# Three edits to a one-layer decoder step: late squares of the second norm, two squares of the first norm summed by TensorE, two projection outputs side by side

## The chip, the cores and the metric

The kernel runs on one core of a Trainium2 chip. The engines are TensorE (PE in the profile; PEld is its weight load), VectorE (DVE), ScalarE (ACT), GpSimd (POOL) and SyncE (SP), which issues most of the loads. Each engine works through its own list of instructions in order and waits for others by semaphores. The metric is the device time of one execution in microseconds, the median of several runs. What a core's memory for matmul results holds is called PSUM; it has eight banks, and a tile of the kernel takes one or two of them.

## The reference, cut to what matters

One layer of a decoder step on 576 tokens (512 of a new sequence, 64 of eight running ones), 1024 channels, all in float32:

```
xn = rms_norm(h, g_mix);  z = xn @ w_in                      # 6 x 1024 columns
h  = h + (gate_a * (conv(...) @ w_out_conv) + gate_b * pool(...)) @ w_o
hn = rms_norm(h, g_mlp)
h  = h + square(relu(hn @ w_up)) @ w_down                    # 4096 wide
h  = h + sigmoid(rms_norm(h, g_ple) @ w_ple_gate) * (p @ w_ple_proj)
return rms_norm(h, g_final), ...                             # and the new states
```

`rms_norm(x, g)` is `x * rsqrt(mean(x * x) + 1e-6) * g`. There are four of these norms. The first and the second are the ones that the change touches.

## The kernel before, in words

Activations lie with the channels on the partitions: eight chunks `xs[j]` of 128 channels by 576 tokens, the tokens in two halves of 288. For accuracy each float32 operand is split into a high and a low part (`split`, lines 88 and 89: ScalarE casts the high part, VectorE subtracts it), and each product takes three matmuls (high x high, high x low, low x high). A weight half, 128 x 512, is loaded by SP into `wraw` (eight buffers), split into `wsp` (NF = 7 slots), and used. `stream.take(n)` hands out the next n halves and sees to it that the splits run up to seven halves and the loads six further ahead; with `live`, it counts halves handed out earlier that are still in use. The halves of `w_up` are partly sums of two loads, the second of them issued from GpSimd's queue (line 149).

A norm is spread over the work around it. The gain g is folded into the operands, and the factor 1/rms per token is applied to the products or to the outputs later. `Rms.add` squares a chunk on ScalarE (line 307) and adds it on GpSimd to the first square (line 311), so that one sum tile remains in `parts`. `Rms.tokens` sums that tile over the partitions with matmuls against a column of ones, one for each of six groups of 96 tokens (line 320, twelve TensorE instructions), takes the root on ScalarE (line 324) and refines its reciprocal on VectorE (lines 325 to 329). `Rms.spread` brings the result back to all partitions with six small matmuls (line 336), and `copies` puts it into SBUF.

First norm (lines 351 to 361): the eight chunks are squared as they arrive, TensorE works through chunk k of the first three products (`psf`), and after k = 5 come the sums, after k = 6 the spreading.

Projection with `w_o` (lines 591 to 602): the operands `merged` are eight split chunks; the last two come out of the pooling gates just before. For each of eight outputs x TensorE runs 48 matmuls (8 chunks x 3 x 2 halves) into two banks. VectorE adds the result to `xs[j]` (line 596), ScalarE applies the gain (`gx`, line 599), and after each second output `hg.add` makes the seven operands of the next stage from the pair (lines 514 to 525, tiles `gx` and `gt`). Then the chunk is squared for the second norm.

MLP (lines 608 to 657): four blocks b of 1024 columns. The product with `w_up` is done with seven quarter products in place of eight (`pairs_of`); one pair is seven quarters of twelve matmuls. In the first block, pair 0 is written in a late order: three of the four chunks are used first, and what needs the last operands (`rest`) comes behind. `finish` applies the squared ReLU and splits the result; `between(q)` runs after pair q and holds, in block 0, the second norm's sums (q = 0) and its spreading (q = 1). Its result `r2s` is used only in the last block (line 654). There are six banks in this stage.

A planner orders each engine's list before the run by costs and the availability of buffers, with program order as its priority. An instruction can so be moved ahead of its place in the text. From the projection on, every matmul issued through the helper `matmul` is kept behind the TensorE instruction that was written before it; the norm's own matmuls are not kept so, but the matmul written next is kept behind them.

Of the kernel before, what the change touches and what calls it, by code (L numbers as in the profile page):

```python
# [9 lines left out]
AF = mybir.ActivationFunctionType  # L10
# [3 lines left out]
D = 1024  # L14
NJ = D // P
# [3 lines left out]
NH = 2  # L19
# [23 lines left out]
def tile_hybrid_step(ctx: ExitStack, tc: tile.TileContext, x, pt, vecs, rc, ident, sconv, spool, w_first, w_in,  # L43
                     w_pool, w_oc, w_o, w_up, w_down, w_pg, w_pp,
                     y_out, ncp, npp, ncs, nps):
    nc = tc.nc
# [19 lines left out]
    def bank():  # L66
        return banks.tile([P, 512], F32, tag="b", name="b")[:, :HT]
# [28 lines left out]
    def split_act(src, scale=None):  # L96
        return split(src, [P, NH, HT], acts, "act", scale)

    def mm(outs, w, c, m, act, start, stop):

        wh, wl = (t[:, c % KH:c % KH + m] for t in w[c // KH])
        for i, (wt, at) in enumerate(((wh, act[0]), (wh, act[1]), (wl, act[0]))):
            for o, cols in outs:
                matmul(o, wt, cols(at), start=start and i == 0, stop=stop and i == 2)

    def both(ps):
        return [(ps[h] if isinstance(ps, list) else ps[:, h, :HT], lambda t, h=h: t[:, h, :]) for h in range(NH)]

    def steps(ps, unit, operands, ks, base=0, m=P, step=P, first=None, last=None):
        for k in ks:  # L110
            mm(both(ps), unit, base + k * step, m, operands[k], k == first, k == last)

    def product(unit, operands, base=0, m=P, step=P):

        ps = psum.tile([P, NH, 512], F32, tag="ps", name="ps") if banks is None else [bank() for _ in range(NH)]
        n = len(operands)
        steps(ps, unit, operands, range(n), base, m, step, 0, n - 1)
        return ps
# [101 lines left out]
    halved = [i + h * NQ for i in range(NQ) for h in range(2)]  # L220
# [16 lines left out]
    stream = Stream(order)  # L237
# [5 lines left out]
    def v(i, j):  # L243
        return vec[:, i, j:j + 1]

    xall = const.tile([P, NJ, NH, HT], F32, tag="xall", name="xall")
    xs = [xall[:, j] for j in range(NJ)]
# [12 lines left out]
    epst = const.tile([P, 1], F32, tag="epst", name="epst")  # L260
# [10 lines left out]
    xg, first = [], []  # L271
# [24 lines left out]
    class Rms:  # L296
# [2 lines left out]
            self.shape = [P, n, width]  # L299
            self.at = [(h, c) for h in range(n) for c in range(0, width, chunk)]  # L300

        def add(self, t, last=False):
            sq = tmp.tile(self.shape, F32, tag="t", name="sq")
            if last:
                nc.vector.tensor_tensor(out=sq, in0=t, in1=t, op=ALU.mult)
            else:
                nc.scalar.activation(sq, t, AF.Square)  # L307
            if last or not self.parts:
                self.parts.append(sq)
            else:  # L310
                nc.gpsimd.tensor_tensor(out=self.parts[0], in0=self.parts[0], in1=sq, op=ALU.add)  # L311

        def tokens(self):

            n, m = len(self.at), self.chunk
            self.ps = ps = psum.tile([P, NH, 512], F32, tag="ps", name="psn")
            sums = ps[:m, 0, self.width:self.width + n]
            for i, (h, c) in enumerate(self.at):
                for k, a in enumerate(self.parts):
                    nc.tensor.matmul(  # L320
                        sums[:, i:i + 1], a[:, h, c:c + m], ones32[:, 0:1],
                        start=k == 0, stop=k == len(self.parts) - 1)
            rt, ms, y, t = (tmp.tile([m, n], F32, tag=g, name=g, bufs=2) for g in ("rt", "ms", "ry", "rz"))
            nc.scalar.activation(rt, sums, AF.Sqrt, bias=epst[:m], scale=1.0 / D)
            nc.vector.tensor_scalar(out=ms, in0=sums, scalar1=1.0 / D, scalar2=EPS, op0=ALU.mult, op1=ALU.add)
            nc.vector.reciprocal(y, rt)
            nc.vector.tensor_tensor(out=t, in0=y, in1=y, op=ALU.mult)
            nc.vector.scalar_tensor_tensor(out=t, in0=t, scalar=-0.5, in1=ms, op0=ALU.mult, op1=ALU.mult)
            nc.vector.scalar_tensor_tensor(out=y, in0=t, scalar=1.5, in1=y, op0=ALU.add, op1=ALU.mult)
            self.y = y  # L330
# [19 lines left out]

    stat = Rms()
    for j in range(NJ):
        stat.add(xs[j])
    ps0 = [psum.tile([P, NH, 512], F32, tag="ps", name="psf") for _ in range(3)]
    for k in range(NJ):
        for u in range(3):
# [51 lines left out]
    for j in range(NJ):  # L408
        ps = product(stream.take(2), xg)
# [5 lines left out]
    for j in range(NJ):  # L415
        ps = product(stream.take(2), ya_in)
# [3 lines left out]
    merged = []  # L420
    for g, w in enumerate(WINDOWS):
        pooled = []
        for i in range(2):
            j = 2 * g + i
            ps = product(stream.take(2), xg)
# [13 lines left out]
            while d < w:  # L439
                q = tmp.tile([P, PEXT], F32, tag="ext", bufs=4, name="q")  # L440
# [23 lines left out]
        for i in range(2):  # L464
            ps = product(stream.take(2), xg)
# [6 lines left out]
        for i in range(2):  # L472
            j = 2 * g + i
            ps = product(wp, pooled, base=i * P, step=2 * P)
            t = tmp.tile([P, NH, HT], F32, tag="t", name="t")
# [15 lines left out]
    def quarter(o, w, bs, ks, start, stop):  # L491
        for k in ks:
            wh, wl = (t[:, k * P:(k + 1) * P] for t in w)
            hi, lo = bs[k]
            for i, (wt, at) in enumerate(((wh, hi), (wh, lo), (wl, hi))):
                matmul(o, wt, at, start=start and k == 0 and i == 0,
                       stop=stop and k == NQ - 1 and i == 2, skip_group_check=True)

    class Operand:

        def __init__(self):
# [25 lines left out]
    def pairs_of(n, op, corner, finish, late=False, between=None):  # L527
# [17 lines left out]
        for i in range(n):  # L545
# [41 lines left out]
            if between:  # L587
                between(i)


    stat = Rms()
    hg = Operand()
    for x, j in enumerate(halved):
        ps = product(stream.take(2), merged)
        for h in range(NH):
            nc.vector.tensor_tensor(out=xs[j][:, h], in0=ps[h], in1=xs[j][:, h], op=ALU.add)
        if x % 2 == 0:
            g = tmp.tile([P, 4, HT], F32, tag="g", name="gx", bufs=2)
        nc.scalar.mul(g[:, 2 * (x % 2):2 * (x % 2) + 2], xs[j], v(G_MLP, j))
        if x % 2:  # L600
            hg.add(x // 2, g)
        stat.add(xs[j])


    accs = [None] * NJ
# [2 lines left out]
    for b in range(NFB):  # L608
        sq = [None] * NJ

        def corner(q, g, c11):
            nc.scalar.activation(g[:, 1], c11, AF.Relu)

        def finish(q, g):
            nc.scalar.activation(g[:, 0], g[:, 0], AF.Relu, scale=-1.0)
            nc.scalar.activation(g[:, 2:4], g[:, 2:4], AF.Relu)
            nc.scalar.activation(g, g, AF.Square)
            sq[q] = split_act(g[:, 0:2])
            sq[q + NQ] = split_act(g[:, 2:4])

        def between(q):
            if b == 0 and q == 0:
                stat.tokens()
            if b == 0 and q == 1:
                stat.r2s = stat.copies(stat.spread(), "r", "rs")[1]

        pairs_of(NQ, hg, corner, finish, b == 0, between)
        r2s = stat.r2s
        if b == NFB - 1:
            pp = []  # L630
            for k in range(2):
                t = tmp.tile([P, NH, HT], F32, tag="t", name="pin")
                nc.sync.dma_start(t, pt[:, k])
                pp.append(split_act(t))
        for j in range(NJ):
            if j == 0:
                two = [stream.take(2), stream.take(2, live=2)]
                two = [(w, [bank() for _ in range(NH)]) for w in two]
                for ks in (halved[:-2], halved[-2:]):
                    for w, ps in two:  # L640
                        steps(ps, w, sq, ks, first=halved[0], last=halved[-1])
            if j < 2:
                ps = two[j][1]
            else:
                ps = product(stream.take(2), sq)
            if b == 0:
                accs[j] = keep.tile([P, NH, HT], F32, tag="keep", name="acc")
                for h in range(NH):
                    nc.scalar.copy(accs[j][:, h], ps[h])
                continue  # L650
            for h in range(NH):
                nc.vector.tensor_tensor(out=accs[j][:, h], in0=ps[h], in1=accs[j][:, h], op=ALU.add)
            if b == NFB - 1:
                nc.vector.tensor_tensor(out=accs[j], in0=accs[j], in1=r2s, op=ALU.mult)
                nc.vector.tensor_tensor(out=xs[j], in0=accs[j], in1=xs[j], op=ALU.add)
                hg2.append(split_act(xs[j], v(G_PLE, j)))
                stat3.add(xs[j])
# [3 lines left out]
    for i in range(2):  # L661
        w = stream.take(2)
        for m in range(NJ // 2):
            ps = product(w, pp, base=2 * m * P)
            t = keep.tile([P, NH, HT], F32, tag="keep", name="proj")
# [25 lines left out]
    for h, (a, b) in enumerate(((0, cut), (cut, NT))):  # L691
        for j in range(NJ):
            if h == 0:
                gate_w.append(stream.take(2))
            ps = psum.tile([P, NH, 512], F32, tag="ps", name="psg")
# [106 lines left out]
```

## Time and profile before

| | |
|---|---|
| median of the runs | 912.74 us (three runs, 911.63 to 913.75) |
| the profiled execution's own time | 914.41 us |
| span of its instructions | 912.6 us |
| TensorE busy | 892.8 us (98%) |
| VectorE, ScalarE, GpSimd busy | 524.6, 375.2, 114.3 us |
| mean granted TensorE clock | 0.987 of full speed |

In the lines of a timeline the columns are start in us, duration in us, engine, source line, operation, written tile and what it reads, shapes, and how many instructions were merged; in brackets stand the idle time of the engine before it and what ended it. A matmul's duration overlaps with the next one's: what it costs is the distance between two starts. In the view by windows the columns are the stretch in us, its length, the busy time and number of instructions of PE, PEld, DVE, ACT and POOL, the granted clock of TensorE, the share of the DMA engines and GB/s.

### The profile page before, as it was taken

Reading aid. Unit: us, or ns where it says so; the run is one execution under the profiler, and the core shown is the slowest. Engines: PE = TensorE matmul, PEld = TensorE weight load, DVE = VectorE, ACT = ScalarE, POOL = GpSimd, SP = SyncE. Lnnn points to the kernel's source line nnn. Section 1 sums busy time; section 2 is a strip of 40 time slices with the busy share of each in tenths; the row PEclk is TensorE's granted clock in tenths of the full one; section 3 lists DMA queues with packets and bytes.
Section 4 is the critical chain, followed back from the end, with each engine's and each line's share of the span. In section 5 each row is a group of like instructions: output and inputs, shape, how many; then the busy total and the mean of one; then the engine's idle time right before and its main releaser. Section 6 shows DMA issues by size and latency. Waiting matters only on the chain.

```text
span 912.6 us, 16574 instructions
## 1 busy us (share of the span) xinstructions
PE 892.8 (98%) x6650; PEld 890.1 (98%) x6650; DVE 524.6 (57%) x880; ACT 375.2 (41%) x642; POOL 114.3 (13%) x150
## 2 busy tenths in 40 slices
PE   8999999999999999999899999999999999999995
PEld 8999999999999999999799999999999999999995
DVE  7654544423335767857785327733773467687555
ACT  8232222322212323344575336721573157546432
POOL 5000000000002211012200110001100110021353
PEclk9999999999999999999799999999999999999997
DMA  8422222222222222333443535444544454333002
GB/s 271 138 83 82 81 82 82 86 89 83 83 82 82 81 82 83 107 96 87 110 127 126 136 96 148 129 104 106 139 137 107 110 123 135 96 98 94 18 23 83
DMA packets 52653, 93.66 MB, mean 103 GB/s; under 512 B 6240, under 2 KB 9952, under 8 KB 52576
## 3 DMA queue, kind: packets, MB, share of 16 engines
q1 hardware_dynamic: 47824, 84.18, 29.3%
q0 software_dynamic: 4608, 8.39, 5.9%
q8 instruction: 52, 0.85, 0.4%
q14 instruction: 25, 0.20, 0.1%
q10 hardware_dynamic: 144, 0.03, 0.0%
HBM read 89.60 MB, written 2.99 MB: 101 GB/s over the span
## 4 chain that ended last, share of the span: by engine, by line
PE 93%; DVE 2%; ACT 2%; DMA 1%; issue 1%; POOL 1%; SPq 0%; DVEq 0%; ACTq 0%; POOLq 0%
PE b L62 47%; PE ps L62 38%; PE psg L62 6%; PE psf L62 1%; DMA xall<-x 1%; ACT hi L88 1%; PE psn L320 1%; PE psn L336 1%; POOL sq L311 0%; ACT hi L91 0%; DMA raw<-w_pg 0%; DVE lo L89 0%; ACT sq L307 0%; DVE gt L523 0%; DVE xall L684 0%
## 5 line engine op out<-in xcount | busy, mean ns | idle before, releaser
L88 ACT CAST hi<-raw 128x512 fp32r<-128x512 f32 x290 | 178.9, 620 | 389.1 <-PE ps L62 206.0
L89 DVE TENSOR_TENSOR lo<-raw,hi 128x512 fp32r<-128x512 f32 x290 | 205.0, 711 | 144.0 <-ACT hi L88 140.4
L62 PE MATMUL b<-lo,hi 128*128 128x288 f32 x1120 | 277.4, 297 | 2.9 <-DVE lo L89 2.9
L62 PE MATMUL b<-hi 128*128 128x288 f32 x1120 | 277.3, 297 | 2.6 <-ACT hi L88 1.6
L62 PE MATMUL b<-hi,lo 128*128 128x288 f32 x1120 | 277.0, 296 | 0.0
L62 PEld LDWEIGHTS b<-lo,hi 128*128 128x128 f32 x1120 | 193.4, 189 | 3.4 <-DVE lo L89 3.4
L62 PEld LDWEIGHTS b<-hi 128*128 128x128 f32 x1120 | 193.4, 189 | 3.1 <-ACT hi L88 1.8
L62 PEld LDWEIGHTS b<-hi,lo 128*128 128x128 f32 x1120 | 193.5, 189 | 0.0
L62 PE MATMUL ps<-hi 128*128 128x288 f32 x880 | 188.5, 296 | 0.0
L62 PE MATMUL ps<-lo,hi 128*128 128x288 f32 x880 | 188.4, 296 | 0.0
L62 PE MATMUL ps<-hi,lo 128*128 128x288 f32 x880 | 188.4, 296 | 0.0
L62 PEld LDWEIGHTS ps<-hi 128*128 128x128 f32 x880 | 141.8, 189 | 0.0
L62 PEld LDWEIGHTS ps<-lo,hi 128*128 128x128 f32 x880 | 141.8, 189 | 0.0
L62 PEld LDWEIGHTS ps<-hi,lo 128*128 128x128 f32 x880 | 141.8, 189 | 0.0
L149 POOL DMA_DIRECT2D raw<-w_up x32 | 27.9, 871 | 326.7 <-DMA raw<-w_up 194.8
L311 POOL TENSOR_TENSOR sq<-sq 128x576 f32<-128x576 f32 (+2 forms) x34 | 44.3, 1303 | 119.6 <-ACT sq L307 70.5
L62 PE MATMUL psg<-hi 128*128 128x320 f32 (+1 forms) x128 | 38.1, 298 | 0.7 <-ACT r L343 0.7
L62 PE MATMUL psg<-lo,hi 128*128 128x320 f32 (+1 forms) x128 | 37.9, 296 | 0.0
L62 PE MATMUL psg<-hi,lo 128*128 128x320 f32 (+1 forms) x128 | 37.9, 296 | 0.0
L89 DVE TENSOR_TENSOR lo<-s,hi 128x512 fp32r<-128x512 f32 x32 | 24.1, 752 | 12.4 <-ACT hi L88 11.6
L169 DVE TENSOR_TENSOR s<-raw 128x512 f32<-128x512 f32 x16 | 12.0, 748 | 32.5 <-DMA raw<-w_up 32.4
L307 ACT ACTIVATE sq<-xall 128x576 f32<-128x576 f32 (+2 forms) x39 | 22.6, 585 | 18.1 <-DVE xall L713 18.1
(124 smaller groups left out, 719.3 us busy)
## 6 DMA issues: line engine op xcount, KB each, us to landing
raw<-w_in SPq DMA_DIRECT2D x90, 256.0 KB, 2.7
raw<-w_up SPq DMA_DIRECT2D x80, 256.0 KB, 2.9
raw<-w_down SPq DMA_DIRECT2D x64, 256.0 KB, 2.9
raw<-w_up POOLq DMA_DIRECT2D x32, 256.0 KB, 4.5
raw<-w_oc SPq DMA_DIRECT2D x16, 256.0 KB, 2.7
raw<-w_o SPq DMA_DIRECT2D x16, 256.0 KB, 2.7
raw<-w_pg SPq DMA_DIRECT2D x16, 256.0 KB, 3.1
xall<-x SPq DMA_DIRECT2D x7, 288.0 KB, 6.1
```

The lines of the kernel that those rows point to most:

```text
L62: i = nc.tensor.matmul(*args, **kw)
L88: nc.scalar.copy(hi, src)
L89: nc.vector.tensor_tensor(out=lo, in0=src, in1=as32(hi), op=ALU.subtract)
L149: nc.gpsimd.dma_start(raw, y, accum_op=ALU.add)
L169: nc.vector.tensor_tensor(out=p.rs2, in0=p.rs1, in1=p.ra, op=ALU.add)
L307: nc.scalar.activation(sq, t, AF.Square)
L311: nc.gpsimd.tensor_tensor(out=self.parts[0], in0=self.parts[0], in1=sq, op=ALU.add)
L320: nc.tensor.matmul(sums[:, i:i + 1], a[:, h, c:c + m], ones32[:, 0:1], start=k == 0, stop=k == len(self.parts) - 1)
L336: nc.tensor.matmul(self.ps[:, h, c:c + m], self.y[:, i:i + 1].broadcast_to([m, P]), idt[:m, :m], start=True, stop=True)
```

## The change: what it does

- First norm: the last two of the eight squares are no longer added by GpSimd. They stay as parts of their own, and `tokens` sums three tiles with TensorE where it summed one.
- Projection: a helper `two_products` makes two products side by side, over all chunks but the last two for both, and then over the last two. The same order stood in the `w_down` loop before and is now a function; it is used also for the first two outputs with `w_o`.
- Second norm: the last two squares are taken out of the projection loop and put behind pair 0 of the first block, `tokens` is put behind pair 1 and the spreading behind pair 2. The two squares and the root are kept behind the ScalarE instruction written before them (`pin`).

```diff
-        def add(self, t, last=False):
+        def add(self, t, last=False, part=False, pin=False):
...
-                nc.scalar.activation(sq, t, AF.Square)
-            if last or not self.parts:
+                i = nc.scalar.activation(sq, t, AF.Square)
+                if pin:
+                    tc.keep_in_program_order(i)
+            if last or part or not self.parts:
                 self.parts.append(sq)
...
-            nc.scalar.activation(rt, sums, AF.Sqrt, bias=epst[:m], scale=1.0 / D)
+            i = nc.scalar.activation(rt, sums, AF.Sqrt, bias=epst[:m], scale=1.0 / D)
+            if pin:
+                tc.keep_in_program_order(i)
...
     for j in range(NJ):
-        stat.add(xs[j])
+        stat.add(xs[j], part=j >= NJ - 2)
...
+    def two_products(operands, ks):
+
+        two = [(w, [bank() for _ in range(NH)]) for w in (stream.take(2), stream.take(2, live=2))]
+        for part in (ks[:-2], ks[-2:]):
+            for w, ps in two:
+                steps(ps, w, operands, part, first=ks[0], last=ks[-1])
+        return [ps for _, ps in two]
...
+    opened = two_products(merged, range(NJ))
     for x, j in enumerate(halved):
-        ps = product(stream.take(2), merged)
+        ps = opened[x] if x < 2 else product(stream.take(2), merged)
...
-        stat.add(xs[j])
+        if x < NJ - 2:
+            stat.add(xs[j])
...
             if b == 0 and q == 0:
-                stat.tokens()
+                for j in halved[-2:]:
+                    stat.add(xs[j], pin=True)
             if b == 0 and q == 1:
+                stat.tokens(pin=True)
+            if b == 0 and q == 2:
                 stat.r2s = stat.copies(stat.spread(), "r", "rs")[1]
...
-                two = [stream.take(2), stream.take(2, live=2)]
-                two = [(w, [bank() for _ in range(NH)]) for w in two]
-                for ks in (halved[:-2], halved[-2:]):
-                    for w, ps in two:
-                        steps(ps, w, sq, ks, first=halved[0], last=halved[-1])
+                two = two_products(sq, halved)
```

More of the change, by code (lines that the diff above doesn't have):

```diff
@@ L311, in add, with tokens @@
                 nc.gpsimd.tensor_tensor(out=self.parts[0], in0=self.parts[0], in1=sq, op=ALU.add)
-        def tokens(self):
+        def tokens(self, pin=False):
             n, m = len(self.at), self.chunk
@@ L636, in tile_hybrid_step @@
             if j == 0:
-                two = [stream.take(2), stream.take(2, live=2)]
-                two = [(w, [bank() for _ in range(NH)]) for w in two]
-                for ks in (halved[:-2], halved[-2:]):
-                    for w, ps in two:
-                        steps(ps, w, sq, ks, first=halved[0], last=halved[-1])
+                two = two_products(sq, halved)
             if j < 2:
-                ps = two[j][1]
+                ps = two[j]
             else:
```

## The prediction

> **What bounds the kernel now.** I read the page's first part, then the clock in windows, then the timelines around the gaps. From the page:
>
> ```profile
> PE 892.8 (98%) x6650; PEld 890.1 (98%) x6650; DVE 524.6 (57%) x880; ACT 375.2 (41%) x642; POOL 114.3 (13%) x150
> ```
>
> TensorE is busy 98% of the span, so only two things can be won: its idle time, 912.6 - 892.8 = 19.8 us in all, and time in which its clock is low. The view by windows (length, busy time and instructions of PE, PEld, DVE, ACT, POOL, then the granted clock) shows where the clock is low:
>
> ```profile
> 22.00:25.40 3.40, 1.52 (x15) 1.52 (x16) 3.40 (x5) 1.55 (x2) 1.83 (x1) 0.96 0.37 122
> 25.40:28.80 3.40, 3.40 (x17) 3.40 (x17) 2.51 (x9) 0.00 (x0) 0.00 (x0) 0.54 0.89 288
> ...
> 441.60:445.00 3.40, 1.38 (x8) 0.79 (x6) 3.12 (x7) 2.82 (x5) 0.78 (x2) 1.00 0.60 198
> 445.00:448.40 3.40, 0.92 (x4) 0.82 (x4) 3.33 (x4) 1.51 (x4) 1.53 (x2) 0.50 0.78 155
> 448.40:451.80 3.40, 3.40 (x20) 3.40 (x19) 2.44 (x4) 2.66 (x4) 0.00 (x0) 0.50 0.15 57
> 451.80:455.20 3.40, 3.40 (x16) 3.40 (x15) 0.44 (x2) 0.62 (x1) 0.88 (x1) 0.50 0.24 77
> ...
> 465.00:470.00 5.00, 5.00 (x40) 5.00 (x39) 4.36 (x9) 2.71 (x7) 0.00 (x0) 1.00 0.72 177
> ```
>
> After 3.4 us with only 1.52 or 1.38 us of PE work, the clock is at half for one stretch at the first norm and for three at the second. The two places in PE's timeline, second norm first:
>
> ```profile
> 441.72 0.29 PE L62 MATMUL b<-hi,lo 128*128 128x288 f32 x1
> 443.62 0.40 PE L62 MATMUL b<-hi 128*128 128x288 f32 x1 [1.60 <-ACT hi L88]
> 444.43 0.40 PE L62 MATMUL b<-lo,hi 128*128 128x288 f32 x1 [0.42 <-DVE lo L89]
> ...
> 447.58 0.61 PE L62 MATMUL b<-lo,hi 128*128 128x288 f32 x1 [2.48 <-DVE lo L89]
> ...
> 448.71 0.44 PE L62 MATMUL b<-hi,lo 128*128 128x288 f32 x1
> 448.95 1.97 PE L320 MATMUL psn<-ones,sq 128*96 128x1 f32 x12
> 450.77 0.59 PE L62 MATMUL b<-hi 128*128 128x288 f32 x1
> ...
> 455.23 0.29 PE L62 MATMUL b<-hi 128*128 128x288 f32 x1
> 455.36 0.29 PE L62 MATMUL b<-lo,hi 128*128 128x288 f32 x1
> ```
>
> Three waits, 4.5 us together, for splits of the last operands of the first pair; then 23 matmuls (counted in the timeline) and the norm's sums run from 447.58 to 455.23 at half clock (0.24 us from start to start, as 448.71 to 448.95; 0.13 at full clock, as 455.23 to 455.36; over longer stretches 0.1325). What makes the operands late:
>
> ```profile
> 434.19 0.45 DVE L523 TENSOR_TENSOR gt<-gx,gt 128x288 f32<-128x288 f32 x1
> ...
> 437.23 0.68 DVE L89 TENSOR_TENSOR lo<-raw,hi 128x512 fp32r<-128x512 f32 x1
> ...
> 438.09 0.67 ACT L307 ACTIVATE sq<-xall 128x576 f32<-128x576 f32 x1
> ...
> 438.66 1.12 ACT L88 CAST hi<-raw 128x512 fp32r<-128x512 f32 x2
> ...
> 438.91 1.42 POOL L311 TENSOR_TENSOR sq<-sq 128x576 f32<-128x576 f32 x1 [4.15 <-ACT sq L307]
> ...
> 439.30 1.59 DVE L89 TENSOR_TENSOR lo<-raw,hi 128x512 fp32r<-128x512 f32 x1 [1.39 <-ACT hi L88]
> ...
> 440.81 0.81 DVE L596 TENSOR_TENSOR xall<-b,xall 128x288 f32<-128x288 f32 x2
> ...
> 442.33 0.67 ACT L307 ACTIVATE sq<-xall 128x576 f32<-128x576 f32 x1
> ...
> 442.91 0.66 ACT L88 CAST hi<-gx 128x576 fp32r<-128x576 f32 x1
> ...
> 444.67 2.19 DVE L523 TENSOR_TENSOR gt<-gx,gt 128x288 f32<-128x288 f32 x1
> ...
> 444.83 1.70 POOL L311 TENSOR_TENSOR sq<-sq 128x576 f32<-128x576 f32 x1
> ```
>
> The squares of the last two chunks stand in ScalarE's queue ahead of the casts TensorE waits for, and each GpSimd addition stretches a VectorE instruction beside it: 0.68 becomes 1.59, and 0.45 becomes 2.19.
>
> **The change part by part.** (1) Late squares. Without the square at 438.09 the weight casts behind it start 438.66 - 438.09 = 0.57 earlier; without the addition at 438.91 the VectorE split takes 0.68 in place of 1.59, 0.91 less. So the last chunk's sum (440.81) and all behind it come 1.48 earlier. The cast at 442.91 also loses the square ahead of it (442.91 - 442.33 = 0.58), ends near 441.4, and TensorE, free at 441.85, no longer has the first wait (1.60). Next is the low part of the same operand: VectorE works without a gap there, so 444.43 only becomes 442.95; a wait of about 1.0 remains. Then the 2.19 becomes 0.45, 1.74 less, and the last resumption, 447.58, becomes 447.58 - 1.48 - 1.74 = 444.36, behind a wait of about 0.9.
>
> The norm's sums leave this place. They come back behind the second pair at full clock, where the first norm's 12 instructions took 24.92 - 23.88 = 1.04 (rows below). What is left here are the 23 matmuls. In 441.6 to 445.0 TensorE now stands 1.9 of 3.4 us, so is busy about 1.5: nearest to 1.38 and 1.52, after which the clock fell. I take one stretch at half clock: 4.8 matmuls until 445.0, 14.2 in the 3.4 us at 0.24, the last 4 in 0.53, end 448.9 instead of 455.23: 6.3 won, less 1.04, **5.3 us**. Bounds: without a fall, 444.36 + 23 x 0.1325 = 447.4, 7.8 less 1.04, 6.8; with a second stretch another 3.4 x (1 - 0.1325/0.24) = 1.5 less, 3.8; and nothing, if other work fills the place (rivals).
>
> The Trainium skill ("TensorE: Matmul & The Clock Gate", Part 1) says that the clock halves after an idle window of about 3.4 us and returns after a busy one. The stretches above agree in length, but the two windows before the falls were not idle, so the rule as it stands is too mild; by it the 6.8 would hold.
>
> (2) What is moved and must be hidden. Two squares (0.67 each), two additions (1.42 and 1.70), the table load and the root go behind the first and second pair; the spreading of the result a pair later, same work. The casts which the squares are pinned behind, and where TensorE needs the sums:
>
> ```profile
> 463.85 0.67 ACT L88 CAST hi<-g 128x576 fp32r<-128x576 f32 x1
> ...
> 470.74 1.47 PE L336 MATMUL psn<-idt,ry 96*128 96x96 f32 x12
> ...
> 474.62 0.67 ACT L88 CAST hi<-g 128x576 fp32r<-128x576 f32 x1
> ```
>
> Squares from 464.5, additions done near 468: 2.7 before TensorE ends the second pair (470.74). The root waits for sums already there; behind it ScalarE's casts stand up to the load's 1.3 longer, covered by weights split ahead. The additions again stretch VectorE, by up to 2 x 1.74 = 3.5 us, in a stretch where it is busy 4.36 of 5; no matmul waits for VectorE there, so I cost it at 0, and at 3.5 if that cover were gone. The Trainium skill ("SBUF — State Buffer", section on the two separate sides) has VectorE and GpSimd share one port pair under an exclusive lock when a VectorE operation has two SBUF inputs; the 2.19 agrees, and by it the price moves with the additions and doesn't vanish. The two loads of the per-layer inputs on SP take the squares' buffers and so shift with them; weight loads behind them run six ahead: 0.
>
> (3) Two squares of the first norm by TensorE.
>
> ```profile
> 17.66 3.77 POOL L311 TENSOR_TENSOR sq<-sq 128x576 f32<-128x576 f32 x2 [1.05 <-ACT sq L307]
> ...
> 21.17 0.43 PE L62 MATMUL psf<-hi,lo 128*128 128x288 f32 x2
> ...
> 21.87 1.96 POOL L311 TENSOR_TENSOR sq<-sq 128x576 f32<-128x576 f32 x1
> ...
> 23.88 1.18 PE L320 MATMUL psn<-ones,sq 128*96 128x1 f32 x12 [2.29 <-POOL sq L311]
> ...
> 24.92 0.65 PE L62 MATMUL psf<-hi 128*128 128x288 f32 x2
> ...
> 28.92 1.48 PE L336 MATMUL psn<-idt,ry 96*128 96x96 f32 x12
> ```
>
> The last two of seven additions go (half the 3.77, and 1.96); the fifth ends near 19.6, before TensorE is free, so the wait of 2.29 goes. But three parts make 36 instructions of 12: 36 x 1.04/12 = 3.12. Start 23.88 - 2.29 = 21.59, end 24.71 against 24.92: **0.2 us**. Whether the clock then falls as before is open: a stretch with twelve such sums and eight matmuls (448.40) did not raise it, so I take that it falls. Bounds: -0.2, by 1.18/12 each; +1.8 if it stays up, since 18 matmuls then take 18 x 0.1325 = 2.4 and not 28.92 - 24.92 = 4.0.
>
> (4) Two projection outputs side by side.
>
> ```profile
> 385.79 0.53 PE L62 MATMUL b<-hi 128*128 128x288 f32 x2 [0.99 <-DVE t L476]
> ...
> 388.41 0.76 DVE L89 TENSOR_TENSOR lo<-t,hi 128x576 fp32r<-128x576 f32 x1 [0.74 <-ACT hi L88]
> ...
> 417.90 0.69 DVE L169 TENSOR_TENSOR s<-raw 128x512 f32<-128x512 f32 x1 [4.68 <-DMA raw<-w_up]
> ```
>
> The last of `merged` is split at 389.2. Before, its first use came 7 x 6 matmuls after 385.79, at 391.4: no wait to win. The 0.99 at 385.79 is for the PSUM read of an earlier product and stays. The first output is complete after 72 + 12 matmuls instead of 48, 4.8 us later; its sum, gain and square are late, then VectorE's 4.68 idle at 417.90 absorbs them. Two weight halves are split up to 4.8 later, with three more ahead. I take 0; bounds -4.8 (carried on, a rival) and +0.99.
>
> Sum: 5.3 + 0.2 + 0 = 5.5 us. The profiled execution took 914.41 us, its span 912.6; changed it should take 908.9. The median of the runs is 912.74, 1.67 below the profiled one, so I forecast **907.2 us**.
>
> **The rivals.** (A) The clock does not fall at the second norm: 6.8 + 0.2 = 7.0, **905.7 us**, and 904.1 if it holds at the first too. For: two short waits with matmuls between, and the windows' phase decides. Against: 1.5 of 3.4 busy. This is what the Trainium skill's rule gives.
> (B) The list of instructions, written again by the planner, puts other casts where the squares stood; only one of the two steps 1.48 and 1.74 comes. TensorE resumes near 446, two stretches at half clock: 3.8 - 1.7 + 0.2 = 2.3, **910.4 us**. For: casts for weights are ready there. Against: they are at most six ahead.
> (C) The lateness of the first output is carried to the last chunk: resumption at 444.36 + 4.8 = 449.2, half clock until 451.8 (11 matmuls), 12 x 0.1325 after it, end 453.4: 1.8 - 1.04 + 0.2 = 1.0, **911.7 us**, within what can be told. For: VectorE runs behind its products. Against: the 4.68.
> (D) Slower: TensorE, whose matmuls are kept in order behind the sums, waits for the late squares. If ScalarE's list holds them until behind the second pair's casts (end 475.3), squares and additions end near 479.1, and TensorE stands from 470.74: 8.4 us, plus 1.5 of half clock, less 5.5: +4.4, **917.1 us**. It is slower by over 0.2% from a wait of 5.8 on, additions ending after 476.5. For: the pin is only a lower bound on their place. Against: by program order they come before all of the second pair.
>
> **How the numbers follow.** Forecast 0.38, A 0.25, B 0.13, C 0.13, D 0.11. A measurement here can tell about 0.2%, 1.83 us, from no change (the three runs span 911.63 to 913.75). Faster: 0.38 + 0.25 + 0.13 = 0.76; same 0.13; slower 0.11. Range: from 904.1, A with both clocks, to 912.3, which takes in B and C with half a run's scatter; D is left out.
>
> **What would show it.** Right for (1): no wait over about 1 us at the second norm, the split at L523 at 0.45, at most one stretch at 0.50; the sums there gone and back near pair two at 1.0. Right for (3): 36 sums from about 21.6 without a wait before them, and a stretch at half clock. Right for (4): the wait of about 1 us before the first projection matmul still there. Wrong: a wait over 2 us before pair one's last operands (B, C), or before the late sums (D).

## The result and the profile after

| | before | changed |
|---|---|---|
| median of the runs beside each other | 913.25 us | 908.36 us |
| ratio, with its 95% interval | | 0.9946 (0.9929 to 0.9963), 4.9 us faster (3.4 to 6.5) |
| the profiled execution's own time, its span | 914.41, 912.6 us | 907.29, 905.5 us |
| mean granted TensorE clock of that execution | 0.987 | 0.995 |

Run a second time beside other kernels (experiment 9), the changed kernel was 6.1 us faster (3.9 to 8.3). Forecast were 5.5 us.

The span of the profiled execution shrank by 7.1 us, more than the runs did. The profile's chain of the work that ended last shows how much of that is the change's. Its piece at the start of the gate products (start, duration, engine, tile, line, count), before:

```profile
847.22 33.46 PE psg L62 x234
...
902.56 1.46 PE psn L320 x6
```

and after:

```profile
841.19 33.46 PE psg L62 x234
...
896.53 0.84 PE psn L322 x6
```

At the gate products the changed kernel is 847.22 - 841.19 = 6.03 us ahead. From there to the end the work is the same in both; the other 1.1 us arises there, where the sums of the last norm ran at half clock in the one execution and at full clock in the other (1.46 against 0.84 for the same six). That is chance: from the gate products to the end it is 65.4 us before and 64.3 after, but 65.15 in a second profile of the changed kernel (experiment 9), in which the gate products start at 842.08, only 5.1 ahead. It is part of why the runs say 5 to 6 and not 7.

The clock in windows after the change, first at the second norm (the last two stretches are new), then at the first:

```profile
441.60:445.00 3.40, 2.84 (x20) 2.38 (x19) 2.60 (x6) 2.28 (x5) 0.67 (x1) 1.00 0.49 79
445.00:448.40 3.40, 3.40 (x26) 3.23 (x25) 3.40 (x8) 2.66 (x6) 0.00 (x0) 1.00 0.28 81
448.40:451.80 3.40, 3.40 (x28) 3.40 (x27) 3.40 (x8) 2.10 (x5) 0.86 (x1) 1.00 0.57 128
451.80:455.20 3.40, 3.40 (x27) 3.40 (x27) 0.73 (x2) 3.37 (x6) 0.00 (x0) 1.00 0.93 236
455.20:460.00 4.80, 4.21 (x33) 4.01 (x32) 4.80 (x6) 3.49 (x7) 3.86 (x3) 1.00 0.41 76
460.00:465.00 5.00, 4.33 (x38) 4.12 (x37) 5.00 (x9) 1.24 (x3) 0.29 (x1) 1.00 0.52 161
...
22.00:25.40 3.40, 3.40 (x38) 3.40 (x38) 3.30 (x8) 1.75 (x3) 0.00 (x0) 0.98 0.89 266
25.40:28.80 3.40, 3.40 (x17) 3.40 (x16) 0.48 (x3) 0.48 (x1) 0.00 (x0) 0.51 0.96 361
```

The three stretches at half clock behind the second norm are gone. The one behind the first norm is still there. New is that TensorE is not busy throughout between 455 and 465, where GpSimd works.

The stretches of this view are not the steps in which the clock changes. In every trace of this case the granted clock changes only at moments that lie a multiple of 3.41 us apart, in the kernel before at 25.13, 28.54, 444.97 and 455.21, and in each execution these moments lie elsewhere. What follows calls the spans of 3.41 us between such moments the clock's own steps.

TensorE's timeline after the change, at the three places:

```profile
21.64 3.14 PE L322 MATMUL psn<-ones,sq 128*96 128x1 f32 x36
24.64 0.50 PE L62 MATMUL psf<-hi 128*128 128x288 f32 x2
...
385.52 0.53 PE L62 MATMUL b<-hi 128*128 128x288 f32 x2 [0.99 <-DVE t L480]
...
441.97 0.29 PE L62 MATMUL b<-hi 128*128 128x288 f32 x1
442.37 0.40 PE L62 MATMUL b<-lo,hi 128*128 128x288 f32 x1
...
443.75 0.40 PE L62 MATMUL b<-hi 128*128 128x288 f32 x1 [0.45 <-ACT g L544]
...
446.25 0.30 PE L62 MATMUL b<-hi 128*128 128x288 f32 x1
...
459.53 0.37 PE L62 MATMUL b<-hi 128*128 128x288 f32 x1 [0.59 <-ACT hi L88]
...
462.02 0.37 PE L62 MATMUL b<-hi 128*128 128x288 f32 x1 [0.67 <-ACT hi L88]
...
463.68 1.10 PE L322 MATMUL psn<-ones,sq 128*96 128x1 f32 x12
464.64 0.38 PE L62 MATMUL b<-hi 128*128 128x288 f32 x1
```

The balance, from these rows and those of before. The matmul at 385.79 before starts at 385.52: 0.27 us ahead after the first norm. The matmul at 455.23 before (the 19th from the start of the fourth quarter) starts at 446.25: 8.98 ahead, 8.71 of it won at the second norm. Two waits in pair 1 take back 1.6 (0.89 and 0.96 from start to start, less 0.13 each). The sums, now behind them, take 464.64 - 463.68 = 0.96. That leaves 8.98 - 1.6 - 0.96 = 6.4, against 6.03 at the gate products; the remaining 0.4 was not traced to rows.

What stretches VectorE and holds TensorE in pair 1, from the timeline of all engines:

```profile
456.55 2.47 DVE L89 TENSOR_TENSOR lo<-g,hi 128x576 fp32r<-128x576 f32 x1
456.62 3.67 POOL L313 TENSOR_TENSOR sq<-sq 128x576 f32<-128x576 f32 x2
...
458.94 0.45 DVE L566 TENSOR_TENSOR g<-b,u 128x288 f32<-128x288 f32 x1
...
459.30 1.60 DVE L89 TENSOR_TENSOR lo<-g,hi 128x576 fp32r<-128x576 f32 x1
...
461.43 0.45 DVE L568 TENSOR_TENSOR g<-b,g 128x288 f32<-128x288 f32 x1
```

Beside the two late additions two splits take 2.47 and 1.60 us. In VectorE's list the reads of two PSUM banks (lines 566 and 568) stand behind them, and end at 459.39 and 461.88. TensorE goes on at 459.53 and 462.02, both times 0.14 later. The timeline names a ScalarE cast as the releaser, but for the first wait that cast also ended only 0.06 before, so which of the two came last cannot be read from this execution alone; in experiment 1 the same wait is put down to line 566.

### The profile page after: what moved, and what is told of

It is laid out like the page before. It is cut to its first block, busy times and chain, and to the rows that moved or that the text cites. A ratio compares the mean times of both kernels' runs of the same rounds, so it can differ in the third digit from the quotient of the medians.

```text
span 905.5 us, 16619 instructions
## 1 busy us (share of the span) xinstructions
PE 890.5 (98%) x6674; PEld 887.7 (98%) x6674; DVE 520.6 (57%) x880; ACT 374.4 (41%) x642; POOL 111.2 (12%) x148
## 4 chain that ended last, share of the span: by engine, by line
PE 93%; DVE 3%; ACT 1%; issue 1%; DMA 1%; SPq 0%; DVEq 0%; ACTq 0%
PE b L62 46%; PE ps L62 39%; PE psg L62 6%; PE psf L62 2%; DVE lo L89 1%; PE psn L322 1%; PE psn L340 1%; DMA raw<-w_up 1%; DMA xall<-x 1%; DVE xall L609 0%; ACT hi L88 0%; DVE gt L534 0%; DVE gt L532 0%; DVE xall L697 0%; ACT sq L307 0%
## 5 line engine op out<-in xcount | busy, mean ns | idle before, releaser
L313 POOL TENSOR_TENSOR sq<-sq 128x576 f32<-128x576 f32 (+2 forms) x32 | 41.1, 1284 | 113.1 <-ACT sq L307 63.8
L89 DVE TENSOR_TENSOR lo<-s,hi 128x512 fp32r<-128x512 f32 x32 | 22.0, 691 | 15.8 <-ACT hi L88 15.1
L89 DVE TENSOR_TENSOR lo<-g,hi 128x576 fp32r<-128x576 f32 x32 | 26.4, 834 | 6.6 <-ACT hi L88 6.6
```

What stands on the lines that cost most here:

```text
L89: nc.vector.tensor_tensor(out=lo, in0=src, in1=as32(hi), op=ALU.subtract)
```

## The experiments

Each was timed against the kernel before, on the same chip. Differences are (1 - ratio) x the median of before.

| kernel | median, us | ratio (95%) | faster by, us |
|---|---|---|---|
| 1 late work of the second norm alone | 907.63 | 0.9942 (0.9927 to 0.9956) | 5.3 |
| 2 first norm alone | 912.42 | 0.9985 (0.9973 to 0.9998) | 1.4 |
| 3 side by side alone | 913.44 | 1.0000 (0.9989 to 1.0011) | 0.0 |
| 4 changed, no late additions | 909.91 | 0.9967 (0.9952 to 0.9981) | 3.0 |
| 5 changed, one part in the first norm | 906.11 | 0.9919 (0.9906 to 0.9932) | 7.4 |
| 6 changed, late work a pair later | 906.16 | 0.9918 (0.9903 to 0.9933) | 7.5 |
| 7 before, last two squares as parts | 909.69 | 0.9963 (0.9951 to 0.9975) | 3.4 |
| 8 edits 5 and 6 together | 905.42 | 0.9918 (0.9905 to 0.9931) | 7.5 |
| 9 changed, again | 906.72 | 0.9933 (0.9909 to 0.9957) | 6.1 |
| 10 before, idle time filled | 909.94 | 0.9963 (0.9946 to 0.9980) | 3.4 |
| 11 edits 5 and 6 without side by side | 904.97 | 0.9916 (0.9889 to 0.9943) | 7.7 |

**1, 2 and 3: each part alone.** The edits are the hunks of the diff, one group at a time.

> The kernel before with the late squares, sums and spreading of the second norm alone (first norm and projection order as before). Theory: the gain is the second norm's; the waits there sink from 4.5 us to under 1 us, no stretch at half clock there, two waits of together 1.6 us in pair 1 behind the late additions; 4.6 us faster than before (the changed kernel's 4.9 less 0.3 for the first norm). Rival: the order side by side has made the instruction lists around the second norm better; then a wait of 1 us or more is still there before the last operands of pair 0, and it is at most 3.5 us faster.

> The kernel before with two squares of the first norm summed by TensorE alone. Theory: 36 sums in 3.1 us take the place of a wait of 2.3 and 12 sums in 1.0; the clock falls to half near 25.4 as before; 0.2 to 0.3 us faster, not to be told from no change by time, and 0.3 earlier at the first product after the norm. Rival: the sums count as work for the clock, it stays up, and it is 1.8 us faster.

> The kernel before with the first two projection outputs side by side alone. Theory: no wait for the last merged operands was there, so nothing is won: within 0.5 us of before; the wait of 1.0 us before the first projection matmul stays. Rival one: the first output's lateness of 4.8 us is carried on to the second norm, 1 us or more slower. Rival two: it gives the lists slack, 1 us or more faster.

The late work alone gives the whole gain (5.3 us; the changed kernel 4.9 and 6.1). Its profile has no stretch at half clock at the second norm and a wait of TensorE in pair 1 that names line 566:

```profile
460.07 0.37 PE L62 MATMUL b<-hi 128*128 128x288 f32 x1 [0.44 <-DVE g L566]
```

The first norm alone is 1.4 us faster with an interval from 0.2 to 2.5. That holds both the 0.2 of the theory and the 1.8 of the rival, so the time doesn't decide. The profiles show that both happen: of the five profiled executions with 36 sums, four have the fall behind them (experiment 2 itself at 24.50), and experiment 6 has not. How often each happens was not measured. The clock can stay up there without the change too: experiment 7 has the old first norm, and its profile has no fall there. Side by side alone is within 1 us of nothing, as expected.

**4: the changed kernel without the late additions.** The two squares stay parts of their own, so TensorE sums three tiles.

```diff
-                    stat.add(xs[j], pin=True)
+                    stat.add(xs[j], part=True, pin=True)
```

> The changed kernel, but the two late squares stay parts of their own (three tiles summed by TensorE), so GpSimd adds nothing in pair 1. Theory: the two waits of pair 1 (1.6 us) come from the two GpSimd additions, which stretch VectorE; they go, while the sums there take 3.1 in place of 0.94: 0.6 us slower than the changed kernel, so 4.3 faster than before. Rival: the waits come from the splits of the weights having less time, now that TensorE is not slowed in pair 0; they stay, and it is 2.2 slower than the changed kernel, 2.7 faster than before.

The rows that answer the question (VectorE's splits beside which the additions ran before; TensorE's sums):

```profile
456.67 0.75 DVE L89 TENSOR_TENSOR lo<-g,hi 128x576 fp32r<-128x576 f32 x1
457.34 0.45 DVE L566 TENSOR_TENSOR g<-b,u 128x288 f32<-128x288 f32 x1
457.71 0.75 DVE L89 TENSOR_TENSOR lo<-g,hi 128x576 fp32r<-128x576 f32 x1
...
462.47 2.97 PE L322 MATMUL psn<-ones,sq 128*96 128x1 f32 x34
```

Both splits take 0.75 and TensorE runs from 448 to the sums without a gap. So the additions cause the waits of pair 1, and not the splits of the weights. By time it is 3.0 us faster than before (1.7 to 4.4): both the 4.3 of the theory and the 2.7 of the rival lie inside. The rows decide what causes the waits; why its gain is 2 to 3 us smaller than the changed kernel's, where the theory had 0.6, they do not show.

**5: one square of the first norm for TensorE instead of two.**

```diff
-        stat.add(xs[j], part=j >= NJ - 2)
+        stat.add(xs[j], part=j >= NJ - 1)
```

> The changed kernel, but with one square of the first norm left to TensorE in place of two (24 sums instead of 36; the sixth addition stays with GpSimd). Theory: the sixth addition ends before TensorE is free for the sums, so no wait comes back and 12 sums less are worth 1.0 us, and up to 1.6 more in executions where the clock then stays up: 1.0 to 2.6 faster than the changed kernel, 6 to 7.5 faster than before. Rival: the sixth addition stretches the splits for the seventh chunk and TensorE waits for these: within 0.5 us of the changed kernel.

```profile
21.32 2.12 PE L322 MATMUL psn<-ones,sq 128*96 128x1 f32 x24
23.30 0.50 PE L62 MATMUL psf<-hi 128*128 128x288 f32 x2
```

No wait before the sums, and 23.30 - 21.32 = 1.98 us for them in place of 3.0: the 1.0 us is there. By the gains over the kernel before (7.4 against 6.1 and 4.9) it is 1.3 to 2.5 us ahead of the changed kernel; the intervals overlap.

**6: the late work one pair later.** Squares behind pair 1, sums behind pair 2, spreading behind pair 3.

```diff
-            if b == 0 and q == 0:
+            if b == 0 and q == 1:
                 for j in halved[-2:]:
                     stat.add(xs[j], pin=True)
-            if b == 0 and q == 1:
+            if b == 0 and q == 2:
                 stat.tokens(pin=True)
-            if b == 0 and q == 2:
+            if b == 0 and q == 3:
                 stat.r2s = ...
```

> The changed kernel with the late squares, the sums and the spreading each one pair later (behind pairs 1, 2 and 3). Theory: it is the density of VectorE's work beside the additions that turns their lock into waits of TensorE (4.8 of 4.8 us busy in pair 1); a pair later it is less dense, the waits of 1.6 us shrink to under 0.5: 1.2 faster than the changed kernel, 6 faster than before. Rival: every pair has the same work and the waits go along with the additions: no difference to the changed kernel.

```profile
463.39 0.45 DVE L566 TENSOR_TENSOR g<-b,u 128x288 f32<-128x288 f32 x1
...
464.49 3.79 POOL L313 TENSOR_TENSOR sq<-sq 128x576 f32<-128x576 f32 x2 [10.85 <-ACT sq L307]
...
465.06 0.45 DVE L568 TENSOR_TENSOR g<-b,g 128x288 f32<-128x288 f32 x1
465.46 1.54 DVE L89 TENSOR_TENSOR lo<-raw,hi 128x512 fp32r<-128x512 f32 x1
466.92 1.91 DVE L171 SCALAR_TENSOR_TENSOR s<-s,raw 128x512 f32<-128x512 f32 x1
```

The waits are gone, and by median the time is better (7.5 us faster than before, interval 6.1 to 8.9, which overlaps with the changed kernel's), as the theory said, but its reason was wrong. VectorE is as dense here (busy 5.00 of 5 us from 465 to 470), and the additions stretch it as much (1.54 and 1.91). What differs is their place in the list: the PSUM read of line 566 is done before the first addition, that of line 568 runs beside it and keeps its 0.45, and what is stretched is work on weights, for which no matmul waits here. In the changed kernel the additions start ahead of both reads.

In this profile the clock stays up behind the first norm. The 36 sums start at 20.63, a microsecond earlier, and fall into two of the clock's own steps (1.4 us of them before 22.04, 1.7 behind it), where the changed kernel's first profile has 2.9 us of them in one:

```profile
22.00:25.40 3.40, 3.40 (x34) 3.40 (x34) 3.30 (x10) 1.01 (x2) 0.00 (x0) 1.00 0.92 292
25.40:28.80 3.40, 3.40 (x30) 3.40 (x29) 0.70 (x2) 1.81 (x3) 0.00 (x0) 1.00 0.80 273
```

**7: squares and additions taken apart.** The kernel before, with the last two squares where they were, but as parts, so that GpSimd leaves these two additions out.

```diff
-        stat.add(xs[j])
+        stat.add(xs[j], part=x >= NJ - 2)
```

> The kernel before, with the last two squares of the second norm left in their place on ScalarE but not added by GpSimd (TensorE sums three tiles there, 36 sums for 12). It separates the additions from the squares. Theory: without the additions the splits stretched beside them take 0.7 and 0.45 in place of 1.6 and 2.2, and the three waits before pair 0's last operands, 4.5 us, sink by about 2.65 to 1.9; the sums there cost 2 to 3.7 more, so the time is 0 to 2 us under before. Rival: the squares ahead of the casts are the cause; the waits stay over 3 us.

```profile
442.24 0.40 PE L62 MATMUL b<-hi 128*128 128x288 f32 x1 [1.05 <-ACT hi L88]
443.06 0.40 PE L62 MATMUL b<-lo,hi 128*128 128x288 f32 x1 [0.42 <-DVE lo L89]
...
444.47 0.40 PE L62 MATMUL b<-lo,hi 128*128 128x288 f32 x1 [0.74 <-DVE lo L89]
```

The three waits are 1.05, 0.42 and 0.74, together 2.2 in place of 4.5 (expected 1.9). So the additions make half of the waits, and above all the long third one; of what is left, 1.05 is for a cast that still has a square ahead of it. It is faster than expected, 3.4 us, although TensorE does 24 sums more: the clock is at half for two of its own steps (from 445.57) in place of three. In this profile it also stays up at the first norm, which the edit does not touch, so part of the gain may be that.

**8 and 11: the versions put together.** 8 is edits 5 and 6 on the changed kernel; 11 is the same without the side-by-side hunk.

> The changed kernel with both edits: one square of the first norm for TensorE, and the late squares, sums and spreading one pair later. Theory: the gains add, 2.2 to 3.8 us faster than the changed kernel, 7 to 8.5 faster than before. Rival: where either has no gain, the smaller sum.

> One square of the first norm for TensorE and the late work of the second norm one pair later, without the two projection outputs side by side. Theory: the order side by side is worth nothing here: 7.5 us faster than before, as with it. Rival: it is worth 0.5 us or more once the waits around it are gone; then under 7.

Both are the fastest by median (905.4 and 905.0) and faster than the kernel before by more than the scatter; ahead of the changed kernel they are by median only. They are not to be told apart from 5 or 6 alone, nor from each other. The gains of 5 and 6 were expected to add to 7 to 8.5; 7.5 is in that range, yet 6 alone has 7.5 as well, so the adding is not shown. Nor does side by side show a worth here: 7.7 without it, 7.5 with it, but the interval of 11 (5.2 to 10.1) would hide half a microsecond.

**9: the changed kernel again.**

> The changed kernel itself, beside the two below on one chip. Theory: 5 us faster than before, as measured first, and 2 us behind the version with the late work one pair later. Rival: the 2 us between them came from the chips and not from the edit; then it is 7 us faster than before.

6.1 us faster than before lies between the two expectations, and its interval (3.9 to 8.3) holds both, so it stays open. On this chip the changed kernel has 906.72 and version 11 has 904.97, 1.8 apart; the intervals overlap. In its profile TensorE waits 0.40 and 0.74 for splits at the second norm, more than in the first profile, and the clock holds all the same:

```profile
442.10 0.40 PE L62 MATMUL b<-lo,hi 128*128 128x288 f32 x1 [0.40 <-DVE lo L89]
...
443.51 0.40 PE L62 MATMUL b<-lo,hi 128*128 128x288 f32 x1 [0.74 <-DVE lo L89]
```

```profile
441.60:445.00 3.40, 1.82 (x10) 1.25 (x10) 2.66 (x6) 1.71 (x4) 0.86 (x1) 1.00 0.51 110
445.00:448.40 3.40, 3.40 (x26) 3.40 (x27) 3.34 (x7) 2.91 (x6) 0.00 (x0) 1.00 0.24 44
```

**10: the clock's share alone.** The kernel before, with nine matmuls of ones on ones in the waits, their results unused.

```diff
                 rest = range(NQ - 1, NQ)
+                fill = psum.tile([P, NH, 512], F32, tag="ps", name="fill")
+                for _ in range(4):
+                    matmul(fill[:, 0, :P], ones32, ones32, start=True, stop=True)
                 quarter(pa, w, op.f["b11"], rest, False, True)
                 g = copied(pa)
+                for _ in range(5):
+                    matmul(fill[:, 0, :P], ones32, ones32, start=True, stop=True)
                 quarter(pd, ws[1], op.f["t3"], rest, False, True)
```

> The kernel before with nine added matmuls on ones, results unused, in the waits of pair 0 (four ahead of the last operands' first matmul, five after it, about 3.6 us of TensorE at full clock). The waits for the operands stay as long as they were; only the idle time is filled. It measures the clock's share by itself. Theory: the stretches at half clock at the second norm go, though the operands come no earlier; 23 matmuls and the sums behind them take 4 us instead of 7.6: 3 to 4 us faster than before. Rival: the matmuls on ones do not hold the clock, or the late operands are all that matters: no faster than before.

TensorE's timeline, then the clock:

```profile
441.04 1.06 PE L62 MATMUL fill<-ones 128*128 128x128 f32 x8
442.83 0.40 PE L62 MATMUL b<-hi 128*128 128x288 f32 x1 [0.74 <-ACT hi L88]
443.66 0.40 PE L62 MATMUL b<-lo,hi 128*128 128x288 f32 x1 [0.42 <-DVE lo L89]
444.03 1.28 PE L62 MATMUL fill<-ones 128*128 128x128 f32 x10
446.95 0.40 PE L62 MATMUL b<-lo,hi 128*128 128x288 f32 x1 [1.51 <-DVE lo L89]
```

```profile
441.60:445.00 3.40, 2.24 (x17) 1.83 (x16) 3.29 (x6) 2.72 (x7) 1.06 (x2) 1.00 0.61 206
445.00:448.40 3.40, 1.89 (x15) 1.68 (x14) 3.37 (x4) 1.87 (x5) 1.27 (x1) 1.00 0.72 144
```

The operands come as late as before (the last of these matmuls 61.98 us behind the first of the projection, 61.79 before), but the clock stays up, and the kernel is 3.4 us faster (1.8 to 4.9). The fillers took 2.3 us, less than the 3.6 I had put on them, and left 2.7 us of waits; that was enough to hold the clock.

## Why the prediction was right, and where it was not

**The sum** (5.5 us) came out, 4.9 and 6.1 in two measurements, but by luck: the clock gave about 1.5 more than forecast (the step between 5.3 and rival A's 6.8), and waits that stood at 0 took 1.6 back.

**(1) The waits** were right in kind, and nearly in size. The casts no longer stand behind squares, line 523 (now 535) takes 0.45, and 7 shows that the additions alone make about half of the waits. The rows of the sums give the 1.48 to the hundredth. The sixth and the last chunk's sum, before:

```profile
429.14 0.81 DVE L596 TENSOR_TENSOR xall<-b,xall 128x288 f32<-128x288 f32 x2
```

(the last is the row at 440.81 that the prediction shows), and after:

```profile
427.60 0.81 DVE L609 TENSOR_TENSOR xall<-b,xall 128x288 f32<-128x288 f32 x2
...
437.79 0.81 DVE L609 TENSOR_TENSOR xall<-b,xall 128x288 f32<-128x288 f32 x2
```

From the one to the other it is 11.67 us before and 10.19 after, 1.48 less. In the first profile the last sum starts 52.3 us after the projection's first matmul instead of 55.0, 1.27 more than forecast, but these 1.27 are there at the sixth chunk already (42.08 instead of 43.35), ahead of the squares that were moved, and they come from the execution and not from the change: in the second profile of the changed kernel (experiment 9) the sixth sum starts after 43.65 us, in experiment 2, whose second norm is the old one, after 41.94. Part of it is when a load of `w_up` lands for which VectorE waits (the row at 417.90: 32.1 us after the projection's first matmul before, 31.4 and 32.3 in the two profiles after).

Of the waits of 1.0 and 0.9 us that I kept, the first is gone in the first profile and the second is 0.27; in experiment 9 they are 0.66 and 0.90 (from start to start, less 0.13). A third, 0.6 in both, stands ahead of the fourth quarter, for the copy at line 544, which I had not seen coming. One thing is the planner's work: in VectorE's list the split of the first `gt` pair now stands ahead of line 535, and the last of these resumptions no longer waits for that line. Rival B had the planner's hand in it, with the wrong sign.

**"I take one stretch at half clock"** is the step that failed. There was none, as in rival A, which has 7.8 us won at this place before the sums come back; 8.7 were won in the first profile and 7.1 in that of experiment 9 (the same matmul of the fourth quarter at 447.37 there, the projection's first at 385.06). I had set 1.5 us busy of 3.4 beside the 1.38 and 1.52 that were followed by a fall. In the first profile TensorE was busy 2.84 in that stretch, with shorter waits than forecast. In experiment 9, with waits near the forecast, it was busy 1.82 there, but the waits are divided over two of the clock's own steps, with 2.27 and 2.97 us of work (from 440.34 and from 443.76), and the clock held. Where the steps lie is what rival A called the windows' phase. Steps with 2.26 and 1.90 held it in experiment 10; it fell behind steps with 1.39 (the kernel before, from 441.56) and 1.75 (experiment 2, from 440.93). So all 1.5 us in one step might well have been followed by a fall; that was not tested. Of the 1.52, moreover, 1.2 were the norm's sums, and these hold the clock badly: behind a step with 2.9 us of them (from 21.89, busy 3.41 by the profile) it fell. The Trainium skill ("TensorE: Matmul & The Clock Gate", Part 1) gives as the condition for a fall an idle window; by that rule the clock holds here, and it did. In the kernel before it fell after 1.39 us of matmuls in 3.41, so the rule read literally is too mild.

**(2) "No matmul waits for VectorE there, so I cost it at 0"** failed as well: 1.6 us, of the 3.5 I had given for the case that the cover is gone. I looked at the weights, which are split ahead, and not at the PSUM reads in the same list, for which the next quarters wait. The Trainium skill's lock ("SBUF — State Buffer", section on the two separate sides) spoke against the change here and was right: two splits took 2.47 and 1.60 beside the additions, 0.75 without (4). The sums took 0.96 for 1.04, and behind the two waits TensorE shows none for the table load, the root or the moved input loads.

**(3)** was right in its rows: sums from 21.64 without a wait, end 24.64 (24.71), and the clock fell as I took it. That it doesn't in some executions was the upper bound. The gain itself is too small to be shown: the 0.27 us at the projection's first matmul (385.52 for 385.79) agrees with the 0.2, but in the other profiles with the old first norm (1, 3, 7, 10) that matmul starts anywhere between 384.85 and 386.60.

**(4)** was right: 0.99 us of wait at the first projection matmul stayed, 3 is at 1.0000. The first output's sum came 4.5 us later (396.86 for 392.34; 4.8 from the projection's first matmul, as forecast), and the second output's was on time again (398.46 for 398.74), long before 417.90. So C did not happen. D neither: the sums at 463.68 did not wait.

## What to carry to other kernels

An instruction off the critical path costs what stands behind it in the list of its engine, and what it stretches on another engine: look at the place, not at the busy share. Moving it costs little only where what follows it there is early; at the new place it is worth trying one step further on. And where TensorE waits shortly, much of the price may be the clock (3.4 us here, experiment 10), which can be bought back by filling the wait. A coincidence of sums is no proof: here the parts had to be compared one by one, and in a second profile, before what belongs to the change came apart from what belongs to the execution.

## What the runs showed that was not expected

Sums of one column over a tile (line 322) look like full work in the profile, yet the clock fell behind a step that they nearly filled (the stretch from 22.0: busy 3.40, then 0.51), and held when they were divided over two steps (experiment 6). Eighteen matmul instructions of 2.3 us in the waits of pair 0 held it. In every trace the clock changes only in steps of 3.41 us that lie differently in each execution, so the same wait can cost more in one execution than in another; the arrival of loads differs as well. The changed kernel ranges from 905.15 to 909.31 us in experiment 9 alone, and a profiled span alone (7.1 us here) overstates or understates a change of this size.
